# A two-layer trunk's MLP: more pairs ahead of the norm, a third pair of weight-part buffers, another order of seven products

## The chip, the cores and the metric

The kernel runs on one core of one Trainium2 chip. The metric is the time of one execution on the device in microseconds (us); the kernel before was timed three times. The core's engines are PE (TensorE, matmuls), DVE (VectorE), ACT (ScalarE), POOL (GpSimd) and SP (SyncE, which here only starts DMAs). Each engine works through its own queue in order and waits on semaphores of the others.

## What is computed

The reference is a trunk of two layers over 1,024 latent tokens (and, in layer 0, 256 context tokens) of width 1,024. A layer is

```python
p = modulate(rms_norm(x, g1), shift1, scale1) @ w_in
mix = concat(mla_attention(p), fourier_mix(p), hyena(p))
x = x + gate1 * (mix @ w_out)
h = modulate(rms_norm(x, g2), shift2, scale2)
x = x + gate2 * (square(relu(h @ w1)) @ w2)      # w1: 1024 x 4096
```

and a last `rms_norm` gives the output. Shifts, scales and gates are `silu(c) @ w_mod + b_mod`. All is fp32. The change touches the second norm, `h @ w1` ("up") and the start of `@ w2` ("down").

## The kernel before, in words

**Products.** Activations are stored transposed, 128 features by up to 512 tokens to a tile. An fp32 product is three matmuls on fp32r parts, high x high, high x low and low x high (`mm3`, L144 to L147). A block of weights of 128 x 1,024 arrives by a DMA of 512 KB (`wload`, L131) and is split in the kernel (`wsplit`, L137): ACT casts the high part `wh` (L140), POOL subtracts it to give the low part `wl` (L141). Both parts have two buffers, taken in turn by every split of the kernel. Raw weights land in a ring of slots ("wr").

**Up** (`up`, L1227 to L1318) works on the 32 output tiles of w1 in 16 pairs and on the 1,024 latent tokens in two halves of 512. For each pair it forms the 2 x 2 block product with seven block products instead of eight (p1 to p7, each 4 x 3 = 12 matmuls of 128x512), with sums of weights (`r41`, `r32`, built by POOL and DVE, L1290 to L1300) and sums of activations (`t1` to `t4`, and `b11`, `b21`, `b22`, all made in the norm). `top(j)` does p1 and p2 from the first weight block A1; then come r41 with p3 and p5, r32 with p7 and p6, and last A2 with p4 alone. In layer 0 each of A1 and A2 also multiplies the context tokens: 24 matmuls of 128x256. Each finished block gets relu (ACT), square (ACT) and a DMA to the DRAM buffer `d_u`.

**The norm** (`norm_blocks`, L1169) makes the operands of up. Its first half (`first`) gives b11 and b21, so that the tops can run; its second half (`second`) gives b22 and t1 to t4 by a chain of DVE, ACT and POOL. The sums of squares behind it are added by DVE (`square_into`, L204 to L208, tile `nacc`) during the out-projection. While `second` runs, `AHEAD` tops are computed ahead (4 in layer 0, 5 in layer 1), their p1 is put to DRAM as `d_s1` and read back in the loop.

**Down** (`down`, L1320) reads the 32 blocks of `d_u` back (`ur`, L1329), splits them (ACT `uh` L154, POOL `ul` L155) and multiplies by w2, whose blocks are split by `wsplit` too. In layer 0 it also computes layer 1's modulation on DVE (`late_modulation`), whose weights `wmod` come through the same ring of raw slots as w2, and through the same queue, SP's.

The order of instructions on each engine is set by the program: a generator for each side job is advanced at fixed points (`tick`) of the main loop, and the compiler's scheduler interleaves by its own estimates.

Of the kernel before, what the change touches and what calls it, by code (L numbers as in the profile page):

```python
# [33 lines left out]
AHEAD = 4, 5  # L34
# [14 lines left out]
def trunk(tc, a):  # L49
# [3 lines left out]
    with ExitStack() as top:  # L53
# [156 lines left out]
        def sums_by(acc, xs):  # L210
# [1017 lines left out]
        def up(l, ops, hx, opening, psp, chain):  # L1228
# [9 lines left out]
            pool = None  # L1238

            def room(name):  # L1240
                return nt(name) if pool is None else pool.tile([128, 512], F32, tag="c", bufs=6, name=name)
# [38 lines left out]
            drain(chain[-1])  # L1280
            for j in range(16):
# [12 lines left out]
                if j == 0:  # L1294
                    pool = opening()
                    slots((pool, "wr2", 4))
                    ring["at"] = 2
                r32 = wroom()
                V.tensor_tensor(r32[:, 512:], r41[:, 512:], a11, op=ALU.subtract)
                V.tensor_tensor(r32[:, :512], a11, a21, op=ALU.subtract)  # L1300
# [19 lines left out]
        def down(l, xT, chunks, pools, psp, late, last_passes):  # L1320
# [3 lines left out]
            def load(hc, us):  # L1324
                for j in range(4):
# [4 lines left out]
                    for c0, (hi, lo) in sorted(u.items()):  # L1330
                        split_sb(hi, lo, w[:, c0 : c0 + hi.shape[1]], G)
# [437 lines left out]
```

## Time and profile before

| | |
|---|---|
| median of 3 runs | 3284.15 us (3278.79 to 3285.74) |
| profiled execution | 3284.59 us, its span 3282.8 us |
| mean granted clock of TensorE | 0.967 of full speed |
| busy share of the span | PE 93%, DVE 59%, POOL 45%, ACT 42% |

The span is the time from the first to the last instruction in the profile; 1.8 us of the execution lie outside it. Times in the trace count from the span's start. Layer 0's up lies at 896 to 1337 us, layer 1's at 2518 to 2888 us. The busy times overlap, so they don't add up to the span.

### The profile page before, as it was taken

The page shows a single profiled execution, that of the slowest core. Times are in us where ns is not written, and L with a number is a line of the kernel's source. Part 1 is how long each engine was busy: PE and PEld are TensorE (multiplying, and loading weights), DVE is VectorE, ACT ScalarE, POOL GpSimd, SP SyncE. Part 2 cuts the span into 40 slices and gives each one's busy share as a digit, 9 for nine tenths or more (in the row PEclk, how much of TensorE's full clock was granted, in tenths as well). Part 3 has the DMA queues.
Part 4 walks back from the last instruction along what each step waited for, and adds up shares of the span by engine and source line. Part 5 has one row for each costly group of instructions (what it writes and reads, how often), then busy time and mean ns, then how long its engine had stood idle before and what let it go on. Part 6 is the DMA issues. An engine that isn't in the chain of part 4 may idle for free. (4 is left out here: it accounts for less than half of the span.)

```text
span 3282.8 us, 42701 instructions
## 1 busy us (share of the span) xinstructions
PE 3041.8 (93%) x15756; PEld 2518.2 (77%) x15756; DVE 1943.5 (59%) x2976; ACT 1367.7 (42%) x2425; POOL 1490.0 (45%) x952
## 2 busy tenths in 40 slices
PE   5999998999889999899999999998999799989998
PEld 1787886887767888788888787787887577778886
DVE  7885679786773232296225635779867754422226
ACT  4324475674443434311112434576754443432113
POOL 6334337542354444555433224347533655564443
PEclk8999998999989999999999998999999899999998
DMA  6454662433433222666213324752343332362223
GB/s 237 156 186 120 203 176 78 127 104 134 140 101 110 90 94 92 239 230 239 71 66 110 107 85 125 221 130 74 81 165 129 114 120 84 107 220 87 90 64 109
DMA packets 165832, 428.09 MB, mean 130 GB/s; under 512 B 37814, under 2 KB 55383, under 8 KB 165368
## 3 DMA queue, kind: packets, MB, share of 16 engines
q1 hardware_dynamic: 152616, 383.61, 36.1%
q0 software_dynamic: 9504, 34.67, 3.5%
q10 hardware_dynamic: 3504, 7.08, 0.6%
q8 instruction: 125, 2.05, 0.3%
q14 instruction: 83, 0.68, 0.1%
HBM read 322.28 MB, written 103.02 MB: 130 GB/s over the span
## 5 line engine op out<-in xcount | busy, mean ns | idle before, releaser
L141 POOL TENSOR_TENSOR wl<-wr,wh 128x1024 fp32r<-128x1024 f32 (+1 forms) x274 | 666.1, 2433 | 1117.0 <-ACT wh L140 1115.1
L140 ACT CAST wh<-wr 128x1024 fp32r<-128x1024 f32 (+1 forms) x274 | 283.8, 1036 | 850.8 <-PE pso L146 357.4
L1124 DVE SCALAR_TENSOR_TENSOR xT<-pso,modc,xT 128x512 f32<-128x512 f32 (+1 forms) x328 | 240.2, 735 | 478.9 <-PE pso L147 478.9
L145 PE MATMUL pso<-uh,wh 128*128 128x512 f32 (+1 forms) x1312 | 488.9, 373 | 15.1 <-ACT uh L154 13.4
L147 PE MATMUL pso<-uh,wl 128*128 128x512 f32 (+1 forms) x1312 | 484.7, 370 | 16.0 <-POOL wl L141 15.8
L146 PE MATMUL pso<-ul,wh 128*128 128x512 f32 (+1 forms) x1312 | 484.3, 369 | 2.7 <-POOL ul L155 2.7
L1024 POOL TENSOR_SCALAR p<-p,st 128x1280 f32<-128x1280 f32 (+1 forms) x144 | 182.4, 1267 | 269.4 <-DVE st L1019 112.7
L147 PEld LDWEIGHTS pso<-uh,wl 128*128 128x128 f32 x1312 | 250.2, 191 | 63.7 <-POOL wl L141 19.1
L145 PEld LDWEIGHTS pso<-uh,wh 128*128 128x128 f32 x1312 | 250.6, 191 | 59.4 <-ACT uh L154 14.0
L146 PEld LDWEIGHTS pso<-ul,wh 128*128 128x128 f32 x1312 | 250.8, 191 | 49.5 <-POOL ul L155 6.1
L155 POOL TENSOR_TENSOR ul<-ur,uh 128x512 fp32r<-128x512 f32 (+1 forms) x160 | 205.2, 1313 | 46.7 <-ACT uh L154 41.4
L151 DVE TENSOR_TENSOR pt<-pst,pt 128x512 fp32r<-128x512 f32 x328 | 214.7, 682 | 11.8 <-ACT pt L150 10.5
L150 ACT CAST pt<-pst 128x512 fp32r<-128x512 f32 x328 | 181.6, 589 | 86.9 <-PE pst L1045 68.2
L146 PE MATMUL psi<-hl,wh 128*128 128x512 f32 (+1 forms) x536 | 198.7, 371 | 5.3 <-POOL hl L248 2.9
L145 PE MATMUL psi<-hh,wh 128*128 128x512 f32 (+1 forms) x536 | 200.5, 375 | 1.8 <-ACT hh L251 1.1
L147 PE MATMUL psi<-hh,wl 128*128 128x512 f32 (+1 forms) x536 | 198.1, 370 | 3.1 <-POOL wl L141 3.1
L1063 PE MATMUL pv<-pt,v 128*128 128x256 f32 x656 | 170.2, 295 | 14.8 <-DVE pt L151 13.5
L1064 PE MATMUL pv<-pt,v 128*128 128x256 f32 x656 | 165.9, 290 | 5.7 <-DVE pt L151 5.6
L1291 DVE TENSOR_TENSOR wr<-wr 128x512 f32<-128x512 f32 x32 | 38.3, 1198 | 219.7 <-POOL wl L141 116.8
L1045 PE MATMUL pst<-ident,p 128*128 128x128 f32 x1024 | 147.3, 278 | 22.0 <-DVE pt L151 10.0
L1011 DVE TENSOR_REDUCE st<-sx 128x1 f32<-128x1024 f32 x128 | 155.7, 1216 | 15.3 <-PE sx L147 14.7
L1017 ACT ACTIVATE p<-sx,st,acol 128x1024 f32<-128x1024 f32 x128 | 153.7, 1201 | 0.0
(412 smaller groups left out, 7653.5 us busy)
## 6 DMA issues: line engine op xcount, KB each, us to landing
wr<-w SPq DMA_DIRECT2D x153, 512.0 KB, 3.6
wr<-wmod SPq DMA_DIRECT2D x64, 512.0 KB, 4.6
d_u<-c SPq DMA_DIRECT2D x128, 256.0 KB, 2.2
ur<-d_u SPq DMA_DIRECT2D x32, 640.0 KB, 7.1
tb<-ftab POOLq DMA_DIRECT2D x34, 512.0 KB, 4.8
wm<-wmod SPq DMA_DIRECT2D x32, 512.0 KB, 3.4
ur<-d_u SPq DMA_DIRECT2D x32, 512.0 KB, 4.0
wr<-wout SPq DMA_DIRECT2D x28, 512.0 KB, 4.1
```

What stands on the lines that cost most here:

```text
L140: S.copy(hi[:, :n], t[:, :n])
L141: G.tensor_tensor(lo[:, :n], t[:, :n], hi[:, :n].bitcast(F32), op=ALU.subtract)
L145: T.matmul(ps, lhsT=lh, rhs=rh, start=first, stop=False)
L146: T.matmul(ps, lhsT=lh, rhs=rl, start=False, stop=False)
L147: T.matmul(ps, lhsT=ll, rhs=rh, start=False, stop=last)
L150: S.copy(hi, ps)
L151: V.tensor_tensor(lo, ps, hi.bitcast(F32), op=ALU.subtract)
L155: (eng or V).tensor_tensor(lo, src, hi.bitcast(F32), op=ALU.subtract)
L1024: G.tensor_scalar(pr, pr, st[:, 5:6], 1.0, op0=ALU.mult, op1=ALU.mult)
L1063: T.matmul(pv[:, :256], lhsT=vt[:, kt, :], rhs=th, start=j == 0, stop=False)
L1064: T.matmul(pv[:, :256], lhsT=vt[:, kt, :], rhs=tl, start=False, stop=j == n - 1)
L1124: V.scalar_tensor_tensor(x, ps[:, : c1 - c0], g, x, op0=ALU.mult, op1=ALU.add)
```

## The change

Seven parts, in the order of the diff. (1) `AHEAD` is 6 and 8. (2) `wsplit` takes its buffers from a list of slots; in up the list has a third pair, in the pool that `opening()` gives, and that pool is now opened before the loop. To make room the ring's slots in that pool go from 4 to 3 and the buffers of `c` from 6 to 5. (3) The adds of the second norm's sums of squares go from DVE to POOL. (4) In the loop p4 (from A2) comes first, then r41 (p3, p5), then r32 (p7, p6); in layer 1 only the half of A2 that p4 reads is split. (5) r41 and r32 are built with one POOL and three DVE operations, one DVE operation fewer for each pair. (6) At the last pair the first 1,024 columns of `d_u[0]` and `d_u[1]` are read into two slots of the ring before down begins, and down casts from them. (7) layer 1's modulation weights come into two buffers of their own, `wm`.

```diff
-AHEAD = 4, 5
+AHEAD = 6, 8
...
-        def wsplit(t, n):
-            hi = P0.tile([128, 1024], F32R, tag="wh", bufs=2, name="wh")
-            lo = P0.tile([128, 1024], F32R, tag="wl", bufs=2, name="wl")
-            S.copy(hi[:, :n], t[:, :n])
-            G.tensor_tensor(lo[:, :n], t[:, :n], hi[:, :n].bitcast(F32), op=ALU.subtract)
+        parts_of = {"at": 0, "slots": [(P0, "", 2)] * 2}
+
+        def wsplit(t, n, n0=0):
+            parts_of["at"] = (parts_of["at"] + 1) % len(parts_of["slots"])
+            pool, tag, bufs = parts_of["slots"][parts_of["at"]]
+            hi, lo = (pool.tile([128, 1024], F32R, tag=u + tag, bufs=bufs, name=u) for u in ("wh", "wl"))
+            S.copy(hi[:, n0:n], t[:, n0:n])
+            G.tensor_tensor(lo[:, n0:n], t[:, n0:n], hi[:, n0:n].bitcast(F32), op=ALU.subtract)
...
-                    square_into(acc, xs[m], nt("sq")[:, : acc.shape[1]], m == 0)
+                    square_into(acc, xs[m], nt("sq")[:, : acc.shape[1]], m == 0, eng)
...
             drain(chain[-1])
+            pool = opening()
+            slots((pool, "wr2", 3))
+            ring["at"] = 2
+            parts_of["slots"] = [(P0, "", 2)] * 2 + [(pool, "2", 1)]
             for j in range(16):
...
-                r41 = wroom()
+                w = wsplit(A2, 1024, 512 if hx is None else 0)
+                p4 = prod(w, 512, "t4")
+                context(w, 2 * j + 1)
+                tick()
+                r41, r32 = wroom(), wroom()
                 G.tensor_tensor(r41[:, 512:], a21, a22, op=ALU.add)
-                V.tensor_tensor(r41[:, :512], a11, a12, op=ALU.add)
-                V.tensor_tensor(r41[:, :512], r41[:, :512], r41[:, 512:], op=ALU.subtract)
+                V.tensor_tensor(r32[:, 512:], r41[:, 512:], a11, op=ALU.subtract)
+                V.tensor_tensor(r41[:, :512], a12, r32[:, 512:], op=ALU.subtract)
+                V.tensor_tensor(r32[:, :512], a11, a21, op=ALU.subtract)
                 w = wsplit(r41, 1024)
...
+                if j == 15:
+                    for k in range(2):
+                        early.append(P0.tile([128, WRAW], F32, tag="wr", bufs=3, name="wr"))
+                        nc.sync.dma_start(out=early[k], in_=d_u[k][:, :SEQ])
                 p3 = prod(w, 0, "b22")
...
+                block(2 * j + 1, 0, u3, p4)
                 block(2 * j, 512, s1, p3)
                 tick()
-                w = wsplit(A2, 1024)
-                p4 = prod(w, 512, "t4")
-                block(2 * j + 1, 0, u3, p4)
-                context(w, 2 * j + 1)
-                tick()
...
-                    nc.sync.dma_start(out=w[:, :te], in_=d_u[hc * 4 + j][:, :te])
+                    if t0 < te:
+                        nc.sync.dma_start(out=w[:, t0:te], in_=d_u[hc * 4 + j][:, t0:te])
...
-                        split_sb(hi, lo, w[:, c0 : c0 + hi.shape[1]], G)
+                        split_sb(hi, lo, (early[j] if c0 < t0 else w)[:, c0 : c0 + hi.shape[1]], G)
...
-                add = sums_by(ac[:, : c1 - c0], [xcol(xT, j, c0, c1) for j in range(ND)])
+                add = sums_by(ac[:, : c1 - c0], [xcol(xT, j, c0, c1) for j in range(ND)], G)
...
+                        def mod_load(src, n):
+                            t = pools[0].tile([128, WRAW], F32, tag="wm", bufs=2, name="wm")
+                            nc.sync.dma_start(out=t, in_=src)
```

**Place 1: ACT in layer 1's norm.** The casts `t1h` to `t4h` (last digit: feature tile 0 to 3) belong to the norm's second half, `wh` are weight splits, `s1` is the copy of a top's p1, `c` relu or square. Before:

```order
L154 CAST t4h1_23144<-t4_23286 128x512
L154 CAST t1h2_23122<-t1_23291 128x512
L154 CAST t3h2_23130<-t3_23295 128x512
L154 CAST t2h2_23138<-t2_23299 128x512
L140 CAST wh_23454<-wr_23450 128x1024
L154 CAST t4h2_23146<-t4_23303 128x512
L154 CAST t1h3_23124<-t1_23308 128x512
L154 CAST t3h3_23132<-t3_23312 128x512
L1269 COPY s1_23352<-psm_23326 128x512
L154 CAST t2h3_23140<-t2_23316 128x512
L1251 ACTIVATE c_23354<-c_23354 128x512
L1245 ACTIVATE c_23354<-c_23354 128x512
```

and in the changed kernel:

```order
L157 CAST t4h1_23145<-t4_23287 128x512
L157 CAST t1h2_23123<-t1_23292 128x512
L143 CAST wh_23447<-wr_23445 128x1024
L157 CAST t3h2_23131<-t3_23296 128x512
L157 CAST t2h2_23139<-t2_23300 128x512
L157 CAST t4h2_23147<-t4_23304 128x512
L157 CAST t1h3_23125<-t1_23309 128x512
L157 CAST t3h3_23133<-t3_23313 128x512
L1272 COPY s1_23353<-psm_23327 128x512
L157 CAST t2h3_23141<-t2_23317 128x512
L143 CAST wh_23487<-wr_23485 128x1024
L1254 ACTIVATE c_23355<-c_23355 128x512
```

Before, the split between t2h2 and t4h2 is that of r41 of pair 0. Now the splits of the top with index 5 (behind t1h2) and of the one with index 6 (behind t2h3) stand inside the norm, and that of index 7 some rows later.

**Place 2: ACT in layer 0's norm.** Before, up to the first split behind the norm:

```order
L154 CAST t2h3_9011<-t2_9245 128x512
L1261 ACTIVATE c_9313<-psm_9288 128x256
L1251 ACTIVATE c_9283<-c_9283 128x512
L1245 ACTIVATE c_9313<-c_9313 128x256
L1245 ACTIVATE c_9283<-c_9283 128x512
L154 CAST t4h3_9019<-t4_9318 128x512
L1269 COPY s1_9354<-psm_9328 128x512
L140 CAST wh_9438<-wr_9409 128x1024
```

and in the changed kernel:

```order
L157 CAST t2h3_9014<-t2_9248 128x512
L1264 ACTIVATE c_9316<-psm_9291 128x256
L1254 ACTIVATE c_9286<-c_9286 128x512
L1248 ACTIVATE c_9316<-c_9316 128x256
L1248 ACTIVATE c_9286<-c_9286 128x512
L143 CAST wh_9465<-wr_9463 128x1024
L157 CAST t4h3_9022<-t4_9321 128x512
L1272 COPY s1_9357<-psm_9331 128x512
```

The split `wh_9465` of the top with index 5 now stands between the last two casts of the norm; before it no weights are split here until t4h3 is cast. The split of the top with index 4 stands 13 rows ahead, behind t4h1.

**Place 3: SP between up and down, layer 0.** `d_u` writes (L1246 before, L1249 now), w2 loads (`wr`), reads of `d_u` (`ur`) and of the residual (`xT`, `xC`). Before:

```order
L1329 DMA ur_12409<-d_u0_103 128x1280
L1246 DMA d_u30_133<-c_12315 128x512
L1246 DMA d_u31_134<-c_12337 128x512
L1246 DMA d_u31_134<-c_12367 128x256
L1329 DMA ur_12423<-d_u1_104 128x1280
L1329 DMA ur_12437<-d_u2_105 128x1280
L1329 DMA ur_12451<-d_u3_106 128x1280
L1339 DMA xT0_12381<-d_x20_95 128x1024
```

and in the changed kernel:

```order
L1249 DMA d_u28_131<-c_12162 128x512
L1249 DMA d_u30_133<-c_12203 128x512
L1249 DMA d_u30_133<-c_12233 128x256
L134 DMA wr_12464<-w2 128x1024
L1249 DMA d_u31_134<-c_12279 128x256
L134 DMA wr_12608<-w2 128x1024
L134 DMA wr_12892<-w2 128x1024
L1339 DMA ur_12404<-d_u0_103 128x256
L1339 DMA ur_12418<-d_u1_104 128x256
L1339 DMA ur_12432<-d_u2_105 128x1280
L134 DMA wr_12712<-w2 128x1024
L1339 DMA ur_12446<-d_u3_106 128x1280
L1249 DMA d_u31_134<-c_12357 128x512
```

The w2 loads have moved ahead of the reads of `d_u`, and the reads of blocks 0 and 1 fetch only the 256 context columns there, since the 1,024 latent columns were read some rows earlier; the read of block 3 stands behind a fourth w2 load.

## Rows read from the trace of the kernel before

**Rows 1.** The page, part 1: busy time, share of the span, instructions
```profile
PE 3041.8 (93%) x15756; PEld 2518.2 (77%) x15756; DVE 1943.5 (59%) x2976; ACT 1367.7 (42%) x2425; POOL 1490.0 (45%) x952
```

**Rows 2.** Granted clock by stretch: from:to, length, busy of each engine (instructions), PEclk, DMA share, GB/s
```profile
880.00:900.00 20.00, 19.66 (x79) 14.81 (x77) 18.14 (x21) 9.32 (x13) 6.17 (x4) 0.97 0.38 133
940.00:980.00 40.00, 29.20 (x129) 22.99 (x128) 30.08 (x31) 19.31 (x33) 26.45 (x15) 0.83 0.33 112
1060.00:1340.00 280.00, 274.87 (x1444) 233.60 (x1442) 79.97 (x113) 115.70 (x189) 121.61 (x54) 1.00 0.29 93
1340.00:1500.00 160.00, 144.42 (x691) 119.04 (x692) 120.95 (x169) 36.03 (x59) 95.45 (x58) 0.95 0.74 266
```

**Rows 3.** Timeline of PE, layer 0 up: start, length, line, instruction [idle before <- releaser]
```profile
895.76 0.40 PE L145 MATMUL psm<-b11h,wh 128*128 128x512 f32 x1
...
1308.96 0.28 PE L145 MATMUL psm<-hh,wh 128*128 128x256 f32 x1
...
1311.79 0.39 PE L145 MATMUL psm<-b11h,wh 128*128 128x512 f32 x1
...
1336.72 0.28 PE L147 MATMUL psm<-hh,wl 128*128 128x256 f32 x1
```

**Rows 4.** Timeline of PE, layer 1 up
```profile
2518.49 0.39 PE L145 MATMUL psm<-b11h,wh 128*128 128x512 f32 x1
...
2568.14 0.79 PE L145 MATMUL psm<-b22h,wh 128*128 128x512 f32 x1 [7.38 <-ACT wh L140]
...
2604.59 0.39 PE L145 MATMUL psm<-t4h,wh 128*128 128x512 f32 x1
...
2607.36 0.39 PE L145 MATMUL psm<-b22h,wh 128*128 128x512 f32 x1
...
2610.34 0.50 PE L147 MATMUL psm<-b22h,wl 128*128 128x512 f32 x1 [2.35 <-POOL wl L141]
...
2887.62 0.40 PE L147 MATMUL psm<-t4h,wl 128*128 128x512 f32 x1
```

**Rows 5.** Waits of PE from 2515 to 2892: who for whom, us, times, longest
```profile
PE psm L147 <- POOL wl L141: 21.1, 20, 2.4
PE psm L145 <- ACT wh L140: 10.1, 4, 7.4
```

**Rows 6.** Timeline of PE, from up to down and in down, layer 0 and layer 1
```profile
1344.20 0.79 PE L145 MATMUL pso<-uh,wh 128*128 128x512 f32 x1 [7.21 <-ACT uh L154]
...
1380.03 0.80 PE L147 MATMUL pso<-uh,wl 128*128 128x512 f32 x1 [2.83 <-POOL wl L141]
...
1488.94 0.80 PE L147 MATMUL pso<-uh,wl 128*128 128x512 f32 x1 [4.50 <-POOL wl L141]
...
2894.20 0.79 PE L145 MATMUL pso<-uh,wh 128*128 128x512 f32 x1 [6.18 <-ACT uh L154]
```

**Rows 7.** Timeline of POOL at layer 0's norm and in its down
```profile
898.87 2.38 POOL L141 TENSOR_TENSOR wl<-wr,wh 128x1024 fp32r<-128x1024 f32 x1 [4.91 <-ACT wh L140]
...
956.23 1.26 POOL L155 TENSOR_TENSOR t2l<-t,t2h 128x512 fp32r<-128x512 f32 x1
...
1470.16 16.42 POOL L155 TENSOR_TENSOR ul<-ur,uh 128x512 fp32r<-128x512 f32 x8
```

**Rows 8.** Timeline of DVE at layer 0's norm
```profile
895.76 0.68 DVE L208 TENSOR_TENSOR nacc<-nacc,sq 128x512 f32<-128x512 f32 x1
...
898.94 2.85 DVE L1177 SCALAR_TENSOR_TENSOR xT<-xT,gsc,rstd 128x512 f32<-128x512 f32 x1
```

**Rows 9.** The page, parts 5 and 6: weight split, loads
```profile
L141 POOL TENSOR_TENSOR wl<-wr,wh 128x1024 fp32r<-128x1024 f32 (+1 forms) x274 | 666.1, 2433 | 1117.0 <-ACT wh L140 1115.1
L140 ACT CAST wh<-wr 128x1024 fp32r<-128x1024 f32 (+1 forms) x274 | 283.8, 1036 | 850.8 <-PE pso L146 357.4
...
wr<-w SPq DMA_DIRECT2D x153, 512.0 KB, 3.6
...
ur<-d_u SPq DMA_DIRECT2D x32, 640.0 KB, 7.1
```

More of the change, by code (lines that the diff above doesn't have):

```diff
@@ L208, in square_into, with sums_by @@
                 (eng or V).tensor_tensor(acc, acc, tmp, op=ALU.add)
[L210 removed]
+        def sums_by(acc, xs, eng=None):
             def after(mg):
                 for m in (2 * mg, 2 * mg + 1):
[L214 removed]
+                    square_into(acc, xs[m], nt("sq")[:, : acc.shape[1]], m == 0, eng)
             return after
@@ L1236, in prod @@
                 return ps
-            pool = None
+            pool, early = None, []
             def room(name):
-                return nt(name) if pool is None else pool.tile([128, 512], F32, tag="c", bufs=6, name=name)
+                return nt(name) if pool is None else pool.tile([128, 512], F32, tag="c", bufs=5, name=name)
             def out(c, m, t0):
@@ L1288, in up @@
                     s1 = top(j, A1)
-                r41 = wroom()
+                w = wsplit(A2, 1024, 512 if hx is None else 0)
[3 more added lines that the diff above has]
+                r41, r32 = wroom(), wroom()
                 G.tensor_tensor(r41[:, 512:], a21, a22, op=ALU.add)
-                V.tensor_tensor(r41[:, :512], a11, a12, op=ALU.add)
-                V.tensor_tensor(r41[:, :512], r41[:, :512], r41[:, 512:], op=ALU.subtract)
+                V.tensor_tensor(r32[:, 512:], r41[:, 512:], a11, op=ALU.subtract)
+                V.tensor_tensor(r41[:, :512], a12, r32[:, 512:], op=ALU.subtract)
+                V.tensor_tensor(r32[:, :512], a11, a21, op=ALU.subtract)
                 w = wsplit(r41, 1024)
[L1294 to L1300, printed above, removed]
+                if j == 15:
+                    for k in range(2):
+                        early.append(P0.tile([128, WRAW], F32, tag="wr", bufs=3, name="wr"))
+                        nc.sync.dma_start(out=early[k], in_=d_u[k][:, :SEQ])
                 p3 = prod(w, 0, "b22")
@@ L1311, in up, with down @@
                 block(2 * j + 1, 512, u3, p5)
+                block(2 * j + 1, 0, u3, p4)
                 block(2 * j, 512, s1, p3)
                 tick()
-                w = wsplit(A2, 1024)
-                p4 = prod(w, 512, "t4")
-                block(2 * j + 1, 0, u3, p4)
-                context(w, 2 * j + 1)
-                tick()
-        def down(l, xT, chunks, pools, psp, late, last_passes):
+            parts_of["slots"] = [(P0, "", 2)] * 2
+            return early
+        def down(l, xT, chunks, early, pools, psp, late, last_passes):
             te = chunks[-1][1] if chunks[-1][1] > SEQ else SEQ
@@ L1325, in load @@
                 for j in range(4):
+                    have = hc == 0 and j < len(early)
+                    t0 = SEQ if have else 0
+                    w = pools[0].tile([128, TT], F32, tag="ur", bufs=3, name="ur") if t0 < te else None
                     u = {c0: tuple(pools[hc % 2].tile([128, c1 - c0], F32R, tag=f"u{c1 - c0}", bufs=16 if c1 - c0 == 512 else 8,
                                              name=f"u{x}") for x in "hl") for c0, c1, _ in chunks}
-                    w = pools[0].tile([128, TT], F32, tag="ur", bufs=3, name="ur")
-                    nc.sync.dma_start(out=w[:, :te], in_=d_u[hc * 4 + j][:, :te])
+                    if t0 < te:
+                        nc.sync.dma_start(out=w[:, t0:te], in_=d_u[hc * 4 + j][:, t0:te])
                     for c0, (hi, lo) in sorted(u.items()):
-                        split_sb(hi, lo, w[:, c0 : c0 + hi.shape[1]], G)
+                        split_sb(hi, lo, (early[j] if c0 < t0 else w)[:, c0 : c0 + hi.shape[1]], G)
                     us.append(u)
@@ L1536, in opening @@
                 return wctx.enter_context(pool_(f"PA{l}", "right"))
-            up(l, ops, hx, opening, psp, [g for _, _, g in todo])
+            early = up(l, ops, hx, opening, psp, [g for _, _, g in todo])
             slots()
@@ L1550, in late_modulation @@
                         load_crow(crow)
-                        yield from modulation(1, crow, (1, 0, 2, 4, 3, 5), lambda s: (0, 1) if s < 2 else (0,))
+                        def mod_load(src, n):
+                            t = pools[0].tile([128, WRAW], F32, tag="wm", bufs=2, name="wm")
+                            nc.sync.dma_start(out=t, in_=src)
+                            return t
+                        yield from modulation(1, crow, (1, 0, 2, 4, 3, 5), lambda s: (0, 1) if s < 2 else (0,), mod_load)
                     late = late_modulation()
@@ L1594, in trunk @@
                 slots((pools[0], "wr2", 2))
-                down(l, xT, chs, pools, psp, late, last_passes)
+                down(l, xT, chs, early, pools, psp, late, last_passes)
         hctx.close()
```

## The prediction

> **What bounds the kernel now.** I read the page first: PE is busy 93% of the span, the other three engines 42 to 59% [rows 1]. So PE sets the time, and a gain must come from the stretches in which PE waits or runs at the lower clock. Next I compared the busy times and the granted clock of the stretches that the change touches. In the middle of layer 0's up (1060 to 1340 us) PE is busy 274.87 of 280 us at full clock [rows 2]; there is nothing to win. Around the norm (940 to 980 us) it is busy 29.20 of 40 us at a clock of 0.83, and from 1340 to 1500 us 144 of 160 us at 0.95 [rows 2].
>
> How much does each up lose in all? One block product is 12 matmuls: from the first t4h matmul at 2604.59 to the next product's first at 2607.36, 2.77 us. The context's 24 small matmuls take 1311.79 - 1308.96 = 2.83 us [rows 3, 4]. A pair of layer 0 is 7 products and 2 context parts: 7 x 2.77 + 2 x 2.83 = 25.05 us, 16 pairs 400.8 us. It ran from 895.76 to 1337.0 [rows 3], 441.2 us: 40 us lost. A pair of layer 1 is 19.39 us, 16 pairs 310.2 us; it ran from 2518.49 to 2888.0 [rows 4], 369.5 us: 59 us lost. The waits of PE say by what: in layer 1, 21.1 us in 20 waits for the low weight parts of POOL and 10.1 us in 4 waits for the high parts of ACT [rows 5]; the rest of the 59 us is mostly the lower clock after such waits.
>
> Why does PE wait for weights in layer 1 all along, and in layer 0 hardly after the norm? A split takes 1.04 us on ACT and 2.43 us on POOL, one behind the other: 3.47 us [rows 9]. With two buffers, the split of block k can start only when PE is done with block k-2, and has the time of block k-1 for itself. That is two products, 5.5 us, for A1, r41 and r32, but in layer 1 one product, 2.77 us, for A2. So whatever comes behind A2 is late, as the wait of 2.35 us behind t4h shows [rows 4]. In layer 0 the context makes A2 as long as the others.
>
> **The change part by part.**
>
> *More tops and the third buffer, layer 1: -29 us.* Before, at about 2590 us, PE had done five tops and four further products: 5 x 5.54 + 4 x 2.77 = 38.8 us of work in 72 us, with one wait of 7.38 us for a split of ACT [rows 4]. By ACT's order (place 1) the splits of the tops 5 and 6 now stand inside the norm, at places that the norm reached before PE needed them, and that of top 7 right behind. I take all eight tops done at 2590 us too: 44.3 us of work. What is left is 310.2 - 44.3 = 265.9 us. From there on a third pair of buffers gives each split the time of two blocks, at least 8.3 us against 3.47 us, so the waits behind A2 go. I add 3 us for a short wait here and there: 2590 + 265.9 + 3 = 2859 against 2888. Bounds: +33 if the 3 us aren't needed and the tops end a little sooner; +15 if the tops end 8 us later and 6 us of waits stay.
>
> *The same in layer 0: -13 us.* The split of top 4 stands behind t4h1; that of top 5 between the norm's last two casts (place 2), so top 5 can't run before the norm's last POOL subtraction of t2, which ended at 956.23 + 1.26 = 957.5 [rows 7]; then comes a split of 2.43 us on POOL, and a top of 8.37 us: 968.5 us. The first A2 waits for about the same time, since its load stands behind the store of an s1 that ACT copies only after the norm; with 3.6 us of DMA and 3.47 us of split [rows 9] it is there at 967 to 969 us. So p4 starts at 969.5, and 400.8 - 6 x 8.37 = 350.6 us are left: 1320, and 4 us for what still waits: 1324 against 1337. Bounds 7 and 17. From there the layer runs as the full-clock stretch before did.
>
> *From up to down, layer 0: -15 us.* PE waited 7.21 us for the first high part of d_u, then 2.83 and 4.50 us for low weight parts, and the clock was 0.95 over 160 us [rows 6, 2], which is 8 us. A read of d_u takes 7.1 us to land [rows 9]. Blocks 0 and 1 are now read early, during the last pair, and their casts stand ahead of its last relus. PE can go through two or three blocks; the fourth read still waits for its buffer behind POOL: I leave 3 us, a gain of 4.2. The w2 loads now stand ahead of the modulation's loads, and the modulation comes in two buffers, so more slowly; DVE was busy 120.95 of 160 us there [rows 2], and POOL's eight low parts of u took 16.42 us, 2.05 each, where one of the same size took 1.26 at the norm [rows 7]. A DVE that works in smaller bursts leaves POOL the room: the 7.3 us of waits go, and half of the 8 us of clock. 4.2 + 7.3 + 4 = 15.5, taken as 15. Bounds 8 (the transition and half of the waits) and 22.
>
> *The same in layer 1: -3 us.* Here the split of down's second weight block uses the buffer of the last r32, which PE holds to the end of p6, and it stands ahead of the early casts on ACT. So the wait of 6.18 us [rows 6] stays nearly whole; bounds 0 and 6.
>
> *The norm's sums on POOL: +4 us.* A 128x512 add took DVE 0.68 us [rows 8]; on POOL an operation of that size takes 1.26 us [rows 7]. The last add is on the path to each norm, and PE waits at the norms in four places (two halves, two layers). The least is 4 x 0.58 = 2.3 us; the most, if each last add lands beside a blocked operation as the DVE one of 2.85 us [rows 8], 4 x 2.17 = 8.7 us. I take 1 us each, nearer to the row of POOL itself.
>
> *Other edits: nothing.* One DVE operation less per pair, and half a split less in layer 1, lie beside PE, which does 19 or 25 us of matmuls a pair while DVE and POOL are busy about half of that. The ring has six slots instead of seven, and a pair takes four; a load so takes the slot of a sum of weights from two pairs ahead, free long before. If that cover is gone, the slower rival below holds.
>
> The sum is -29 - 13 - 15 - 3 + 4 = -56 us. The profiled execution took 3284.6 us, 0.4 above the median, so the changed kernel comes out at **3228 us**. The bounds of the terms, thought independent, give 3216 to 3247 for this case alone.
>
> **Does one rule speak against it?** A POOL split of 2.38 us began at 898.87, and the DVE operation that began at 898.94 took 2.85 us, where an add of its size took 0.68 [rows 7, 8]: on operands in SBUF the two engines exclude each other. So moving sums to POOL gives DVE no free time; it holds DVE up for longer. In the out-projection before layer 0's norm DVE is busy 18.14 of 20 us [rows 2], and it also empties PE's accumulators there. If DVE is the limit, 35 adds (7 for each of five column chunks) that each cost it 1.26 instead of 0.68 us add 20 us, and with 1.75 us, midway between a free add and a blocked one, 37 us. That is the first rival. The Trainium skill, page "SBUF — State Buffer", section "SBUF: two separate sides", says that the pair of ports shared by VectorE and GpSimd is an exclusive lock held for the whole instruction, the other fully blocking; the two rows agree. Against the rival: PE was busy 19.66 of the same 20 us, so DVE kept up, and I count no more than the last adds.
>
> **The rivals.**
>
> *The sums block DVE* (chance 0.10): 20 to 37 us on top of the sum, so 3248 to 3265; 3255. It would show as PE waiting for DVE in the out-projection.
>
> *The extra tops are worth nothing* (chance 0.20): they stand in ACT's and POOL's queues behind operations of the norm that are late themselves, and p4, now first in the loop, needs t4, the norm's last result; so PE waits at the norm as before. Then only the third buffer and the transition gain. Of layer 1's 29 us, 5.5 came from tops; with 8 us of new waiting there it gives 15, layer 0 nothing: -15 - 15 - 3 + 4 = -29, 3255 us. For it: POOL and DVE exclude each other, and the norm's second half has no reserve.
>
> *Nearly all that was lost comes back* (chance 0.16): both ups lose only 12 us each at the norm (28 and 47 gained), and the transitions give their upper bounds, 22 and 6, with the least cost of the sums: -101 us, 3184; half-way to it from my sum is 3206.
>
> *The ring is too short* (chance 0.04): if the loads of a pair can start only when the r32 before is split, the chain load 3.6, add 1.26, three DVE operations at 0.68, split 3.47, in all 10.4 us, has only p7 and p6 and p4, 8.3 us, to hide behind in pairs without a top of their own, and up to 5 us more when POOL and DVE block each other. At 2.1 to 7 us for each of 32 pairs, 67 to 220 us, it eats the whole gain: 3295 us at the least. It decides from 1.8 us a pair on. Against it speaks the order of the slots above.
>
> **How the numbers follow.** My case has 0.46, the rivals 0.10, 0.20, 0.16 and 0.04; the other 0.04 is for costs that together come to within 0.2% of the time before. 0.2% is 6.6 us, about what a measurement of this kernel tells from no change. So faster 0.92, same 0.04, slower 0.04. For 8 in 10 the range takes my case, the first two rivals and half of the third: 3202 to 3258 us.
>
> **What would show it.** In the changed profile layer 1's up lasts about 340 us instead of 369.5, with the waits for low weight parts nearly gone after the norm; layer 0's about 428 instead of 441; PE's first matmul of down in layer 0 waits about 3 us, in layer 1 about 6. I am wrong if the waits behind A2 are still there, if the norm takes the gain back, or if PE waits for DVE ahead of the norm.

## The result, and the profile after

The changed kernel takes 3234.68 us (median of 4 runs, 3230.63 to 3240.07), the kernel before, timed beside it, 3284.94 us (4 runs, 3278.79 to 3290.96). The ratio is 0.9848 with a 95% interval of 0.9825 to 0.9872: 50 us, or 1.5%, faster. The forecast was 3228 with a range of 3202 to 3258.

The profiled execution has a span of 3232.2 us, 50.6 us less than before. PE does the same matmuls and is busy 94% of it; the first part of the changed kernel's page reads, beside [rows 1]:

```profile
PE 3028.6 (94%) x15756; PEld 2516.0 (78%) x15756; DVE 1884.2 (58%) x2909; ACT 1364.2 (42%) x2425; POOL 1514.3 (47%) x987
```

To find where the 50.6 us come from I cut both spans at points that the change leaves in place: the first product of each layer's up, its last, and the first product of down. This is PE's timeline of the changed kernel (its lines are 3 further down: L148 to L150 are the three matmuls of a product), beside [rows 3, 4, 6]. The 970.33 and 2574.07 rows are the first matmul of p4, behind the last top:

```profile
894.75 0.40 PE L148 MATMUL psm<-b11h,wh 128*128 128x512 f32 x1
...
970.33 0.40 PE L148 MATMUL psm<-t4h,wh 128*128 128x512 f32 x1
...
1322.05 0.40 PE L150 MATMUL psm<-t2h,wl 128*128 128x512 f32 x1
...
1322.29 0.62 PE L148 MATMUL pso<-uh,wh 128*128 128x512 f32 x2
...
1325.27 0.50 PE L149 MATMUL pso<-ul,wh 128*128 128x512 f32 x1 [2.36 <-POOL ul L158]
...
2498.46 0.40 PE L148 MATMUL psm<-b11h,wh 128*128 128x512 f32 x1
...
2574.07 0.40 PE L148 MATMUL psm<-t4h,wh 128*128 128x512 f32 x1
...
2841.28 0.40 PE L150 MATMUL psm<-t2h,wl 128*128 128x512 f32 x1
...
2845.26 1.22 PE L148 MATMUL pso<-uh,wh 128*128 128x512 f32 x2 [3.58 <-ACT uh L157]
```

| stretch (us) | before | after | change | forecast |
|---|---|---|---|---|
| start to layer 0's up | 895.8 | 894.8 | -1.0 | |
| layer 0's up | 441.2 | 427.5 | -13.7 | -13 |
| from its end to layer 1's up | 1181.5 | 1176.2 | -5.3 | -15 |
| layer 1's up | 369.4 | 343.1 | -26.3 | -29 |
| from its end to the end | 394.9 | 390.7 | -4.2 | -3 |

Every wait in layer 1's up now lies before 2565 us, inside the norm. PE's waits from 2495 to 2842 (compare [rows 5]: 21.1 us in 20 waits and 10.1 us in 4):

```profile
PE psm L150 <- POOL wl L144: 7.3, 4, 2.8
PE psm L148 <- ACT wh L143: 4.8, 2, 3.3
```

These are the waits for weights. Beside them PE waits 7.6 us there for the norm's own operands (4.3 us in the kernel before).

The same stretches as in [rows 2], moved to the changed kernel's times, show where the time is still lost: not in the steady part, which runs without a gap, but around the norm and in down.

```profile
880.00:900.00 20.00, 18.43 (x77) 13.95 (x76) 16.68 (x16) 10.01 (x14) 11.18 (x6) 1.00 0.33 107
940.00:980.00 40.00, 34.22 (x179) 29.08 (x178) 27.82 (x22) 20.53 (x35) 26.19 (x15) 0.91 0.43 137
1060.00:1320.00 260.00, 260.00 (x1358) 221.16 (x1357) 62.53 (x97) 106.56 (x174) 110.73 (x50) 1.00 0.30 97
1322.00:1482.00 160.00, 152.40 (x753) 126.95 (x753) 110.84 (x157) 40.03 (x66) 95.96 (x59) 0.97 0.69 250
```

### The profile page after: what moved, and what is told of

The parts are those of the page before. It is cut to its first block, busy times and chain, and to the rows that moved or that the text cites. A ratio compares the mean times of both kernels' runs of the same rounds, so it can differ in the third digit from the quotient of the medians.

```text
span 3232.2 us, 42677 instructions
## 1 busy us (share of the span) xinstructions
PE 3028.6 (94%) x15756; PEld 2516.0 (78%) x15756; DVE 1884.2 (58%) x2909; ACT 1364.2 (42%) x2425; POOL 1514.3 (47%) x987
## 3 DMA queue, kind: packets, MB, share of 16 engines
q8 instruction: 125, 2.05, 0.3%
## 5 line engine op out<-in xcount | busy, mean ns | idle before, releaser
L144 POOL TENSOR_TENSOR wl<-wr,wh 128x1024 fp32r<-128x1024 f32 (+2 forms) x274 | 650.0, 2375 | 990.7 <-ACT wh L143 985.5
L143 ACT CAST wh<-wr 128x1024 fp32r<-128x1024 f32 (+2 forms) x274 | 277.8, 1014 | 846.7 <-PE pso L149 385.0
L1127 DVE SCALAR_TENSOR_TENSOR xT<-pso,modc,xT 128x512 f32<-128x512 f32 (+1 forms) x328 | 239.5, 735 | 468.3 <-PE pso L150 436.4
L148 PE MATMUL pso<-uh,wh 128*128 128x512 f32 (+1 forms) x1312 | 488.5, 374 | 13.5 <-DVE xT L1127 5.2
L150 PE MATMUL pso<-uh,wl 128*128 128x512 f32 (+1 forms) x1312 | 483.6, 369 | 4.1 <-POOL wl L144 4.1
L148 PEld LDWEIGHTS pso<-uh,wh 128*128 128x128 f32 x1312 | 250.5, 191 | 59.7 <-DVE xT L1127 7.5
L150 PEld LDWEIGHTS pso<-uh,wl 128*128 128x128 f32 x1312 | 250.3, 191 | 49.3 <-POOL wl L144 5.0
L158 POOL TENSOR_TENSOR ul<-ur,uh 128x512 fp32r<-128x512 f32 (+1 forms) x152 | 197.4, 1328 | 66.3 <-ACT uh L157 61.4
L171 DVE SCALAR_TENSOR_TENSOR junk<-wm,crow 128x1024 bf16<-128x1024 f32 x128 | 193.4, 1533 | 38.3 <-DMA wm<-wmod 37.5
L148 PE MATMUL psi<-hh,wh 128*128 128x512 f32 (+1 forms) x536 | 201.7, 377 | 1.8 <-ACT hh L254 1.1
L150 PE MATMUL psi<-hh,wl 128*128 128x512 f32 (+1 forms) x536 | 198.2, 370 | 3.0 <-POOL wl L144 3.0
L1066 PE MATMUL pv<-pt,v 128*128 128x256 f32 x656 | 172.1, 297 | 15.2 <-DVE pt L154 13.9
```

Of the source, the lines that this page charges most:

```text
L143: S.copy(hi[:, n0:n], t[:, n0:n])
L144: G.tensor_tensor(lo[:, n0:n], t[:, n0:n], hi[:, n0:n].bitcast(F32), op=ALU.subtract)
L148: T.matmul(ps, lhsT=lh, rhs=rh, start=first, stop=False)
L150: T.matmul(ps, lhsT=ll, rhs=rh, start=False, stop=last)
L158: (eng or V).tensor_tensor(lo, src, hi.bitcast(F32), op=ALU.subtract)
L171: V.scalar_tensor_tensor(jk, w, 1.0, crow[:, st, :], op0=ALU.mult, op1=ALU.mult, accum_out=modc[:, l, st, n : n + 1])
```

## Experiments

Each kernel below differs from the changed one or from the one before by the edit shown. Stretches are read from its PE timeline at the same points as in the table above. "Wait" is PE's idle time ahead of layer 0's down, "down" runs from that down's first product to its last. Behind it, to layer 1's up, the same operations take 699.1 us in the kernel before, 700.4 in the changed one and 691.7 to 701.2 in the others, so this stretch is left out of the comparisons. Each stretch is read from one execution, and the runs of one kernel lie up to 10 us apart, so a microsecond or two in this table decides nothing by itself.

| kernel | median us | ratio to before (95%) | layer 0's up | wait | layer 0's down | layer 1's up |
|---|---|---|---|---|---|---|
| before | 3284.94 | 1 | 441.2 | 7.2 | 475.2 | 369.4 |
| changed | 3234.68 | 0.9848 (0.9825-0.9872) | 427.5 | 0.0 | 475.8 | 343.1 |
| e1, tops 4 and 5 | 3260.72 | 0.9920 (0.9905-0.9935) | 442.7 | 3.2 | 474.9 | 355.1 |
| e2, two part buffers | 3261.98 | 0.9924 (0.9909-0.9939) | 433.0 | 5.0 | 473.0 | 369.3 |
| e3, p4 last | 3236.25 | 0.9844 (0.9828-0.9860) | 427.9 | 1.4 | 476.5 | 344.3 |
| e4, sums on DVE | 3225.53 | 0.9816 (0.9800-0.9833) | 425.4 | 0.0 | 474.7 | 340.0 |
| e5, modulation in the ring | 3240.40 | 0.9864 (0.9842-0.9885) | 428.2 | 0.0 | 485.6 | 343.9 |
| e6, one buffer for it | 3228.16 | 0.9825 (0.9809-0.9842) | 427.5 | 0.2 | 471.7 | 344.7 |
| e7, before + third buffer | 3270.86 | 0.9955 (0.9938-0.9971) | 433.9 | 18.4 | 471.8 | 346.3 |
| e8, before + tops 6 and 8 | 3293.39 | 1.0019 (1.0006-1.0032) | 443.2 | 7.0 | 477.2 | 381.0 |
| e9, no modulation | 3219.22 | 0.9795 (0.9774-0.9816) | 428.2 | 0.0 | 463.9 | 344.3 |
| e10, no early reads | 3240.10 | 0.9857 (0.9841-0.9872) | 427.5 | 6.7 | 475.4 | 344.1 |
| e11, e4 and e6 together | 3220.93 | 0.9796 (0.9779-0.9813) | 426.9 | 0.0 | 469.5 | 339.0 |
| e12, e11 with p4 last | 3220.19 | 0.9801 (0.9786-0.9815) | 425.7 | 1.4 | 469.8 | 340.1 |

### The tops and the third buffer, each taken away and each alone

```diff
e1 (from the changed kernel)
-AHEAD = 6, 8
+AHEAD = 4, 5
e2 (from the changed kernel)
-            parts_of["slots"] = [(P0, "", 2)] * 2 + [(pool, "2", 1)]
e7 (from the kernel before: wsplit of the change, and at pair 0)
-                    slots((pool, "wr2", 4))
+                    slots((pool, "wr2", 3))
+                    parts_of["slots"] = [(P0, "", 2)] * 2 + [(pool, "2", 1)]
e8 (from the kernel before)
-AHEAD = 4, 5
+AHEAD = 6, 8
```

e1:

> The changed kernel with AHEAD back at 4 and 5. My account (the tops fill the time of the norm): p4 is first in the loop and needs the norm's last operand, so PE idles from the last top to it. Layer 0's up 427.5 -> about 441 us (+13), layer 1's 343.1 -> about 352 (+9), the rest unchanged: about 3257 us. Rival (the extra tops are worth nothing, the third buffer carries all): both ups within 4 us of the changed kernel, 3235 to 3240.

Measured 3260.72 us; the ups take 442.7 and 355.1 us, 15.2 and 12.0 more than in the changed kernel. The rival falls, and PE idles where the account says, 19.97 us in layer 0 and 22.49 us in layer 1:

```profile
967.43 0.79 PE L148 MATMUL psm<-t4h,wh 128*128 128x512 f32 x1 [19.97 <-ACT wh L143]
```

But the norm's last operand isn't what ends this wait. DVE finished the last part of t4 at 959.60; the split of A2 came 7.8 us later, since ACT had waited for its load until 966.33. So with p4 first the tops are what PE does until the norm is done and A2 is loaded and split.

e2:

> The changed kernel with two pairs of part buffers instead of three. My account (a split has only the time of the block before it, and A2 is one product in layer 1): the waits behind A2 come back, 0.5 to 2 us a pair; layer 1's up 343.1 -> 355 to 362 us, layer 0's +1 to +3: 3248 to 3257 us. Rival (the new order and the half split of A2 are enough, the buffer is not needed): layer 1's up at most 347, 3235 to 3240 us.

Measured 3261.98 us, some 5 above the upper end of the account's range; layer 1's up takes 369.3 us, 26.2 more, layer 0's 5.5 more. The wait has the place that was expected, behind p4. PE's timeline, a pair with its own top:

```profile
2701.73 0.40 PE L150 MATMUL psm<-t4h,wl 128*128 128x512 f32 x1
...
2702.46 0.50 PE L148 MATMUL psm<-b22h,wh 128*128 128x512 f32 x1 [0.33 <-ACT wh L143]
...
2704.91 0.50 PE L150 MATMUL psm<-b22h,wl 128*128 128x512 f32 x1 [1.25 <-POOL wl L144]
```

p4's last matmul starts at 2701.73, and the next block waits 0.33 us for its high part and 1.25 us for its low part. This comes back with every pair that has its own top: the next such wait is at 2724.01, 21.6 us on, where 19.4 us of matmuls lie between. So 2.2 us are lost a pair, more than the 1.6 us of the two waits; that is 18 of the 26.2 us, in eight pairs. Most of the rest, 5.5 us, lies in the pairs whose top was done ahead.

e7:

> The kernel before with the third pair of part buffers in up (and the smaller ring that makes room for it), nothing else. Account from the removal of the buffer, which cost 26 us in layer 1 and 5.5 in layer 0: the steady waits go but the norm's waits stay: layer 1's up 369.4 -> 345 to 352, layer 0's 441.2 -> 436 to 441; 3258 to 3268 us. Rival (the buffer helps only with the new order and the half split): layer 1's up 362 or more, 3276 or more.

Measured 3270.86 us, 3 above the account's range. The ups do as the account says, 433.9 and 346.3 us, so the rival falls: the buffer needs neither the new order nor the half split. But 30 us less in the two ups make only 14 us less in span (3268.4 us): 11.2 us in layer 0 and 10.4 us in layer 1 (a wait of 16.59 us instead of 6.18) are lost again where down begins. PE's first product of layer 0's down, and SP's queue before it:

```profile
1346.86 0.79 PE L148 MATMUL pso<-uh,wh 128*128 128x512 f32 x1 [18.38 <-ACT wh L143]
```

```profile
1336.59 0.32 SPq L1334 DMA_DIRECT2D ur<-d_u  x1
1336.96 0.42 SPq L1344 DMA_DIRECT2D xT<-d_x  x1
1337.43 0.42 SPq L1344 DMA_DIRECT2D xC<-d_x  x1
1337.90 0.61 SPq L1344 DMA_DIRECT2D xT<-d_x  x1
1338.56 0.60 SPq L1344 DMA_DIRECT2D xC<-d_x  x1
1339.21 0.45 SPq L134 DMA_DIRECT2D wr<-w  x1
```

The w2 block that the first product waits for is fetched only at 1339.21, behind the reads of d_u and four reads of the residual (xT, xC); in the kernel before, the first product waited for its part of d_u [rows 6], not for w2. Its cast followed at 1345.76. In layer 1 the first product waits for the cast of a w2 block too. The edit moved this load in SP's order without touching the code that issues it; why the scheduler put it there stays open. In the changed kernel the w2 loads stand ahead of these reads (place 3), so the same buffer costs nothing there.

e8:

> The kernel before with AHEAD 6 and 8, nothing else. Here p3, which needs only b22, is first in the loop, so PE had work at the norm without the extra tops. Account (tops fill the norm's time in any order): layer 0's up 441.2 -> 430 to 434, layer 1's 369.4 -> 360 to 364, 3268 to 3275 us. Rival (they pay only where p4 comes first): both within 4 us, 3281 to 3288 us.

Measured 3293.39 us, with a ratio of 1.0019 (1.0006 to 1.0032): the other way than the account, and 5 us above the rival. Layer 0's up is no shorter (443.2 us), and layer 1's longer (381.0 against 369.4). From the last top on PE waits 29.0 us for low parts:

```profile
PE psm L147 <- POOL wl L141: 29.0, 20, 6.2
```

```profile
2631.18 0.79 PE L147 MATMUL psm<-b22h,wl 128*128 128x512 f32 x1 [6.19 <-POOL wl L141]
```

```profile
2627.05 1.78 POOL L1290 TENSOR_TENSOR wr<-wr 128x512 f32<-128x512 f32 x1 [5.16 <-DMA wr<-w]
2628.79 5.16 POOL L141 TENSOR_TENSOR wl<-wr,wh 128x1024 fp32r<-128x1024 f32 x2
```

A pair whose top is done ahead gives PE only five products, 13.9 us, for three splits and the sums of weights. With two buffers these pairs are the ones that lose: the low part for 2631.18 stood on POOL behind the next pair's sum of weights, which itself waited 5.16 us for its load. From the first p3 of layer 1 on, seven such pairs take 117.9 us where their products alone need 97.0; in the changed kernel, with three buffers, seven take 97.7. So moving tops ahead takes from the later pairs the matmuls that hid their splits and loads. With two buffers this costs as much as the filled norm gives, or more. (That the other waits of the 29.0 us come about like the one followed here is argued, not shown.)

### The order of the products

```diff
e3 (from the changed kernel)
-                w = wsplit(A2, 1024, 512 if hx is None else 0)
-                p4 = prod(w, 512, "t4")
-                context(w, 2 * j + 1)
-                tick()
                 r41, r32 = wroom(), wroom()
...
                 block(2 * j, 512, s1, p3)
                 tick()
+                w = wsplit(A2, 1024, 512 if hx is None else 0)
+                p4 = prod(w, 512, "t4")
+                block(2 * j + 1, 0, u3, p4)
+                context(w, 2 * j + 1)
+                tick()
```

> The changed kernel with p4 again last in the loop, all else kept. My account (buffers and tops carry the gain, the order nothing): both ups within 4 us of 427.5 and 343.1, total within 6 us of 3234. Rival (the order removes the waits behind A2): layer 1's up 355 us or more, 3247 us or more.

Measured 3236.25 us, both ups within 1.2 us. With three buffers and the tops, the order of the products is worth nothing that can be measured. (The half split of A2 stays in this kernel.)

### The sums on POOL

```diff
e4 (from the changed kernel)
-                add = sums_by(ac[:, : c1 - c0], [xcol(xT, j, c0, c1) for j in range(ND)], G)
+                add = sums_by(ac[:, : c1 - c0], [xcol(xT, j, c0, c1) for j in range(ND)])
```

> The changed kernel with the sums of squares of the second norm back on DVE. My forecast had +4 us for the sums on POOL, so 4 us less here (3231). The changed trace shows a wait of 3.89 us for the sum in layer 0 where it was 2.45, but up begins 1 us earlier: by that the sums cost nothing, and this kernel is within 3 us of 3235. Rival (the sums block DVE): 20 us less, 3215.

Measured 3225.53 us, 9 us less than the changed kernel (0.9816 against 0.9848; the intervals overlap by 0.0008). All three expectations miss. In its trace 0.7 us of that are won before layer 0's up, 2.1 us in it, 3.1 us in layer 1's up: 5.9 us where the norms are. The other 6 us of the span lie elsewhere, most of them in the stretch that varies anyway, so the sums cost 6 us by the stages and 9 by the medians. Why do sums that DVE has room for cost more on POOL? The timelines of ACT, POOL and PE in the changed kernel, where PE waits 3.89 us at 873.85 for the finished sum (the last row is the kernel before, where it waits 2.45 us, for DVE):

```profile
869.68 0.63 ACT L209 ACTIVATE sq<-xT 128x512 f32<-128x512 f32 x1
```

```profile
870.22 2.36 POOL L144 TENSOR_TENSOR wl<-wr,wh 128x1024 fp32r<-128x1024 f32 x1
...
872.53 1.26 POOL L211 TENSOR_TENSOR nacc<-nacc,sq 128x512 f32<-128x512 f32 x1
```

```profile
873.85 1.87 PE L225 MATMUL psn<-ones,nacc 128*128 128x2 f32 x8 [3.89 <-POOL nacc L211]
```

```profile
875.57 1.05 PE L222 MATMUL psn<-ones,nacc 128*128 128x2 f32 x8 [2.45 <-DVE nacc L208]
```

The square (sq) is there at 870.31. The last add, 1.26 us, starts only at 872.53, behind a weight split of 2.36 us in POOL's queue. And beside DVE the adds take longer: two at 902.53 took 3.38 us, 1.69 each. The other direction shows too, though not where the rival had it: PE waits for no emptied accumulator before the norm. But the norm's own work on DVE is held up. In the changed kernel two of its operations, beside a split (893.27, 2.83 us) and an add (896.06, 1.74 us) on POOL, take 4.57 us:

```profile
893.78 4.57 DVE L1180 SCALAR_TENSOR_TENSOR xT<-xT,gsc,rstd 128x512 f32<-128x512 f32 x2
```

In e4, with POOL free, two of them at 893.46 and 894.72 take 0.73 and 0.74 us. PE then waits 2.9 us for the low parts of b11 and b21 in layer 0, in e4 0.6 us; in layer 1 it waits 7.6 us for the norm's operands, in e4 3.6 us.

### What became of the gain in layer 0's down

```diff
e5 (from the changed kernel)
-                        yield from modulation(1, crow, (1, 0, 2, 4, 3, 5), lambda s: (0, 1) if s < 2 else (0,), mod_load)
+                        yield from modulation(1, crow, (1, 0, 2, 4, 3, 5), lambda s: (0, 1) if s < 2 else (0,))
e6 (from the changed kernel)
-                            t = pools[0].tile([128, WRAW], F32, tag="wm", bufs=2, name="wm")
+                            t = pools[0].tile([128, WRAW], F32, tag="wm", bufs=1, name="wm")
e9 (from the changed kernel)
-                        yield from modulation(1, crow, (1, 0, 2, 4, 3, 5), lambda s: (0, 1) if s < 2 else (0,), mod_load)
+                        V.memset(modc[:, 1], 0.5)
+                        V.memset(gsc[:, 1], 0.5)
+                        yield
e10 (from the changed kernel)
-                if j == 15:
+                if j == 99:
```

e10:

> The changed kernel without the early reads of the first two blocks at the last pair. Account: the first wait of down comes back, 7 us in layer 0 (0 now) and 6 in layer 1 (3.8 now): 3240 to 3246 us. Rival (the order with p4 first has already moved the last writes ahead, so the reads need not be early): 3232 to 3237 us.

Measured 3240.10 us. In layer 0 a wait of 6.7 us is back, in layer 1 it is 4.0 us where the changed kernel has 3.6: the early reads give some 7 us in layer 0 and next to nothing in layer 1. There the casts of these blocks stand behind a split that waits for its w2 load; this is ACT in the changed kernel, and the casts follow at 2844.59:

```profile
2843.64 1.05 ACT L143 CAST wh<-wr 128x1024 fp32r<-128x1024 f32 x1 [6.22 <-DMA wr<-w]
```

So in layer 0 the transition gave what the forecast wanted of it (4.2), and more. Something behind it must take the gain back. In the changed kernel the list of PE's waits in layer 0's down, from 1322 to 1600, has a releaser that [rows 6] did not show:

```profile
PE pso L148 <- DVE xT L1127: 5.2, 5, 3.5
PE pso L149 <- POOL ul L158: 3.8, 4, 2.4
PE pso L148 <- DVE xC L1127: 3.8, 3, 1.6
```

DVE empties PE's accumulators (xT, xC, L1127), and the modulation's operations (L171, 128x1024) stand between in the same queue. PE's longest wait for it, then DVE's timeline ahead of it, and a row from later on, where DVE itself waits:

```profile
1443.33 0.58 PE L148 MATMUL pso<-uh,wh 128*128 128x256 f32 x1 [3.53 <-DVE xT L1127]
```

```profile
1426.08 1.22 DVE L171 SCALAR_TENSOR_TENSOR junk<-wm,crow 128x1024 bf16<-128x1024 f32 x1
...
1429.03 3.42 DVE L171 SCALAR_TENSOR_TENSOR junk<-wm,crow 128x1024 bf16<-128x1024 f32 x1
...
1432.38 1.40 DVE L1127 SCALAR_TENSOR_TENSOR xT<-pso,modc,xT 128x512 f32<-128x512 f32 x2
1433.70 2.23 DVE L171 SCALAR_TENSOR_TENSOR junk<-wm,crow 128x1024 bf16<-128x1024 f32 x1
...
1435.87 2.30 DVE L171 SCALAR_TENSOR_TENSOR junk<-wm,crow 128x1024 bf16<-128x1024 f32 x1
...
1438.10 2.30 DVE L171 SCALAR_TENSOR_TENSOR junk<-wm,crow 128x1024 bf16<-128x1024 f32 x1
...
1440.34 2.27 DVE L171 SCALAR_TENSOR_TENSOR junk<-wm,crow 128x1024 bf16<-128x1024 f32 x1
...
1442.54 0.74 DVE L1127 SCALAR_TENSOR_TENSOR xT<-pso,modc,xT 128x512 f32<-128x512 f32 x1
...
1508.97 3.08 DVE L171 SCALAR_TENSOR_TENSOR junk<-wm,crow 128x1024 bf16<-128x1024 f32 x1 [1.24 <-DMA wm<-wmod]
```

```profile
1431.33 12.41 POOL L158 TENSOR_TENSOR ul<-ur,uh 128x512 fp32r<-128x512 f32 x6
```

From 1400 to 1440, first the changed kernel, then the kernel before:

```profile
1400.00:1440.00 40.00, 39.80 (x201) 33.25 (x199) 39.40 (x56) 5.99 (x9) 17.17 (x8) 1.00 0.60 212
```

```profile
1400.00:1440.00 40.00, 40.00 (x209) 34.02 (x208) 40.00 (x56) 6.89 (x12) 28.03 (x14) 1.00 0.64 231
```

Beside a free POOL such an operation takes 1.22 us, beside POOL's low parts of u 2.2 to 2.3 us, and once, behind a split, 3.42 us; POOL's six at 1431.33 took 12.41 us, 2.07 each, at the same time. From 1400 to 1440 DVE is busy 39.40 us of 40. That alone is not the cause: the kernel before has DVE busy 40.00 of 40 there, and PE no gap. What differs is the order. Four operations of the modulation stand in a row here, and from 1433.78 to 1442.54, 8.76 us, no accumulator is emptied; while the kernel before works on the modulation it never has more than two in a row, and at most 5.59 us without emptying one. The other seven waits for DVE, 5.5 us in all, lie from 1487 to 1539, where DVE waits for single loads of wmod (0.5 to 1.5 us each), with accumulators queued behind the wait. Some of the operations there are stretched beside POOL as well, so the share of the loads in the 5.5 us isn't separated.

e9:

> The changed kernel without the computation of layer 1's modulation: no loads of wmod in down, and constants in place of its results (so the numbers of layer 1 differ; its operations are the same). It measures what the modulation costs PE in layer 0's down in all. From the first product of down to layer 1's up the changed kernel takes 1176.2 us. If the waits for DVE there (9.0 us by the list of PE's waits) and the clock behind them (0.93 over 50 us, 3.5 us) are all the modulation's: about 1163 us, total 3221 to 3224. If PE's waits there have another cause: within 3 us of 1176.

Measured 3219.22 us in 2 runs. From the first product of down to its last the changed kernel takes 475.8 us, this one 463.9: the modulation costs PE 11.9 us there, about the 9.0 us of waits and 3.5 us of clock, and its list of PE's waits names DVE nowhere in down. The stretch of the expectation, to layer 1's up, is 1156.8 us, 6 below what I expected; the rest of the difference lies behind down, in the stretch that varies between kernels.

e5:

> The changed kernel with the modulation's weights again in the ring that w2 uses. From the end of layer 0's up to the 88th accumulator that DVE empties in down (some 230 us later, where the offsets between kernels have settled) the kernel before took 235.6 us and the changed one 229.0; I had forecast 15 us less than before, 220.6. My account of the miss (two buffers make DVE wait in its queue for each load, and PE's accumulators stand behind it): without them DVE goes through the modulation sooner, but POOL and the w2 loads are late as before: 229 to 234 us, total 3235 to 3240. Rival (the two buffers alone cost the 8 us): 221 us, total 3227.

Measured 238.8 us for the stretch and 3240.40 in all: worse than the account's upper end of 234, at its end in total, and the rival falls. From its first product to its last down takes 485.6 us here, 475.8 with the two buffers, and 475.2 in the kernel before, which had waited 7.2 us first. PE's waits up to 1603 have changed their releaser:

```profile
PE pso L150 <- POOL wl L144: 9.3, 3, 6.6
PE pso L148 <- ACT wh L143: 6.0, 3, 3.3
```

None is for DVE. The casts of w2 wait for their loads (18.94 us of ACT's idle time before 1415.51, 19.05 before 1435.61). So the buffers of its own are what took away the waits for weight parts, and they put waits for DVE in their place. Without them the modulation would have eaten the whole gain of the early reads and 3 us more; with them it ate all but 6.6.

e6:

> The changed kernel with one buffer for the modulation's weights instead of two, which spreads the modulation over about twice as many output tiles of down. If DVE's crowding (39.40 us busy of 40 from 1400 to 1440) is what PE waits for, the stretch falls to 221 to 225 us and the total to about 3229. If DVE's wait for each single load is what costs, one buffer makes it worse: more than 232 us, 3238 or more.

Measured 3228.16 us, the total that was expected if the crowding counts, though the interval overlaps that of the changed kernel. From 1400 to 1440 DVE is busy 28.21 us of 40, and PE has no gap there:

```profile
1400.00:1440.00 40.00, 40.00 (x207) 33.74 (x206) 28.21 (x39) 6.23 (x10) 16.75 (x9) 1.00 0.37 128
```

The stretch to the 88th accumulator says the opposite: counted as for the other kernels it rises from 229.0 to about 233.8 us, which was to show that the waits for loads cost. It was the wrong measure, since it ends with an operation of DVE. DVE now waits 106 us in down for loads of wmod (23 us with two buffers), but accumulators are emptied between the loads. What counts is PE, whose waits for DVE in down fall from 9.0 to 5.4 us:

```profile
PE pso L148 <- DVE xT L1127: 3.1, 1, 3.1
PE pso L148 <- DVE xC L1127: 2.3, 1, 2.3
```

Both of these come behind a wait of DVE for a load (2.52 and 3.81 us). From its first product to its last, down takes 471.7 us, 4.1 less than with two buffers; e11 below is 5.2 less than e4 by the same edit. So the long row of operations is gone, and the waits for loads cost a part of what is left: the experiment doesn't choose between the two readings, both have a share.

### Together

e11 is e4 and e6 in one kernel, e12 has e3's order as well.

> The changed kernel with the sums on DVE and one buffer for the modulation. The two gained 10 and 7 us alone, in different places: 3217 to 3220 us if they add up, 3224 to 3226 if only the sums count.

Measured 3220.93 us (5 runs), ratio 0.9796 (0.9779 to 0.9813) to the kernel before, 14 us under the changed kernel's median: the two nearly add up (9.2 and 6.5 us by the medians of e4 and e6).

> The same with p4 last in the loop. The order cost nothing before (3236 against 3235), so within 4 us of the run before this one; if p3 first is of use while the norm ends, 3 to 5 us less.

Measured 3220.19 us, the same within the interval; the order is of no use here either. e11 is the change without one of its seven parts and with one number changed. It and e12 can't be told apart, and they are the fastest versions that still compute the modulation.

## Why the prediction was right

The time lies 7 us above the forecast and inside its own case's range (3216 to 3247). The mechanisms of both ups held: third buffer and tops. (Two slips in its sums change nothing: bounds taken as independent give about 3218 to 3246, and the rival of the short ring multiplies by 32 pairs a cost that it gives only to pairs without a top of their own, of which there are 14.) By its steps:

*Layer 1's up, -29:* it gave -26.3 with the sums on POOL in it, and -29.4 without them (e4). The tops ended 75.6 us after the start where I had 71.5, and the rest took 267.4 us where I had 268.9. The steady part was read rightly from one number: a block of 2.77 us can't hide a split of 3.47 us.

*Layer 0's up, -13:* -13.7; without the sums -15.8. The first p4 came 75.6 us after the start; I had 73.7. That the load of A2 would come late was read rightly too: e1 shows it as what ends the wait.

*From up to down, layer 0, -15:* this is the step that failed, by a factor of three. -5.3 us were measured: -6.6 from the wait and down itself, and +1.3 from the varying stretch behind it. The early reads gave more than the 4.2 us of the forecast. What failed is the sentence that a DVE which works in smaller bursts leaves POOL the room, so that 7.3 us of waits and half of the clock's 8 us go. The waits for low weight parts did go, 9.0 us in three waits between 1340 and 1600. But e5 shows that the modulation's own buffers did that, not room on POOL, whose low parts of u took 2.07 us each as before (2.05). Those for low parts of u grew from 1.4 to 3.8 us, and 9.0 us of waits for DVE came, 3.5 behind four operations of the modulation in a row and 5.5 where DVE waits for its loads. At their worst DVE's bursts were longer than before, not smaller. e9, without the modulation, shows what it still costs: 11.9 us. I had looked at DVE's 120.95 of 160 us [rows 2] as POOL's problem and not asked what else stands in DVE's queue: the accumulators of PE.

*Layer 1's transition, -3:* -4.2 to the end; the wait was 3.58 us instead of nearly all of 6.18. e10 shows that the early reads are not the reason: without them it is 3.99. Nor was it p6 that held up the split, as the forecast had it: p6's last matmul starts at 2841.28, and the cast at 2843.64 came with its w2 load. So the number is right by luck; what shortened the wait stays open.

*The sums, +4:* 6 us in the stages, 9 by the medians. The price of 1 us in four places was too low. I priced the add itself, and neither the split ahead of it in POOL's queue nor the norm's own operations on DVE, which POOL's adds and splits hold up. The rival "the sums block DVE" (20 to 37 us) is refuted in its size and place: before the norm PE waits for no accumulator. Its mechanism is there in small, at the norm itself.

*Other edits, nothing:* right for the order of the products (e3: +1.6 us by the medians). The sums of weights with one operation less, the half split of A2 and the smaller ring were not taken away one by one; that they are worth nothing is not shown for each. It was not asked in the forecast whether the tops alone are worth anything. They are not: e8 is slower than the kernel before. By the medians of the removals the tops are worth 26 us and the buffer 27, together more than the whole gain; put alone into the kernel before, the tops cost 6 to 7 us and the buffer gives 15 to 16 (medians and ratios). The rival "the extra tops are worth nothing" is right for the kernel before and wrong for this one.

## What to carry to other kernels

Where one engine's blocks alternate in length, compare the preparation of a block not with the mean but with the shortest block before it: one short block per round is enough to stall a double buffer, and work that is moved ahead makes more of them. Where a side job shares a queue with the operations that free PE's accumulators, count how many of its operations stand in a row between two of those, and whether it waits for loads there. How full the queue is did not tell: DVE was busy 40.00 of 40 us in the kernel before without a wait of PE. One buffer was 4 to 5 us better than two here. And a small operation moved to a less busy engine is priced with what stands ahead of it in that queue, and with what it holds up on the engine that it left.

## What was not expected

How far DVE and POOL stretch each other: the modulation's 128x1024 operation took 1.22 us alone and up to 3.42 us (1429.03) while POOL was at a split (1428.27, 3.10 us), POOL's 128x512 subtraction 2.07 us where 1.26 was its time at the norm [rows 7]. And how much an untouched stretch moves: the 691.7 to 701.2 us behind layer 0's down are the same operations in all kernels, and still they differ by 9.5 us.
